# Sliding attention of block 2 with heads taken in pairs, skip factors loaded as rows, and other start addresses for block 2's tiles

## The chip, the core and the metric

One core of a Trainium2 chip runs the whole program. TensorE (PE; its weight loads are shown as PEld) multiplies, VectorE (DVE), ScalarE (ACT) and GpSimd (POOL) do the rest, and SyncE (SP) issues most of the weight transfers. SBUF is the on-chip memory of 128 partitions, PSUM the accumulators that TensorE writes. The metric is the device time of one launch in microseconds, the median of three runs.

## The reference

Block 1 is a mixer (mLSTM and differential attention) and a mixture of 32 experts; block 2 has two layers, each a gated feed-forward (ffn1), a mixer of three branches, and a second feed-forward (ffn2). Sequence 256, width 1024, fp32. The changed branch is the third one:

```python
def swa_sink_attention(q, k, v, sinks, band_bias, band_mask):   # 16 query heads, 2 key heads, width 64
    ...                                                          # blocks of 128 queries, window 128
    s = jnp.einsum('bnqkgd,bnskd->bnkgqs', q, kb) * (ATT_HEAD_DIM ** -0.5)
    s = jnp.where(band_mask[None, :, None, None], s + band_bias, NEG)
    m = jnp.maximum(jnp.max(s, axis=-1, keepdims=True), sink)
    e = jnp.exp(s - m)
    p = e / (jnp.sum(e, axis=-1, keepdims=True) + jnp.exp(sink - m))
    o = jnp.einsum('bnkgqs,bnskd->bnqkgd', p.astype(v.dtype), vb)
```

In the mixer, `ssd_mixer` adds `xs * d_skip` per head, and `x = x + rmsnorm(sum(sigmoid(gate) * (branch @ w_branch)) @ w_out)` closes it.

## The kernel before, in words

**Products.** Large products run in a single-pass format (fp32r): each operand is split into a high part (rounded by ACT) and a low part (the rest, by DVE), and three products are summed: high by high, high by low, low by high. Weights arrive in 1 MB pieces in the buffers `raw` or `fraw`; `split_to` makes `wh` and `wl` from them, four pairs of buffers deep. `wstat` holds a weight as the stationary operand and streams the 256 tokens (`xTH`, `xTL`, or a branch's output `yyH`, `yyL`, `yaq`, `yacsB`): a unit is 24 matmuls of 256 columns. `xstat` holds tokens and streams weights: matmuls of 512 columns, as in the second half of a feed-forward (`acc<-wh,fhH`) and in the heads of the stages (`mm<-own,xTH`). In a matmul's name `out<-a,b` a is streamed and b is stationary. Small products in full fp32 show as two records each.

**Order.** Every engine's order is the order in which the program is written. In the mixer a foreground loop of `wstat` units is interleaved with background generators (`ssd`, `swa`, `ret`, one after another). After each unit `bg` asks a running count of estimated TensorE, DVE and ACT work whether the first generator may go on by a step; `need` forces it on.

**`swa` before.** An item is (key head kv, query block b, half i): i picks partitions 0 to 63 or 64 to 127 of `aq` and `ak`, since two heads lie above each other. The eight items go through four stages, one step apart: `logits` (matmuls of one half, then DVE adds the band bias and takes the maximum), `exps` on ACT, `turn` (transposes on TensorE, ACT copies to `pT`, DVE the reciprocal of the sum), and `value` (the transposed weights stationary, 64 columns of `avr` streamed, DVE multiplies by the reciprocal into `ao`). At the end 16 transposes on TensorE turn `ao` over, and it is split into `yyH` and `yyL`. Stages take accumulators from `acc`, a ring of four PSUM banks.

**Addresses.** Each pool lays its tiles one behind another in SBUF, rounded up to 32 B. Small tiles (`dsk` 32 B, `hb` 192 B, `ssc` 16 B) thus set where the large ones behind them start. Start address modulo 128 B, in the program before: `wh`, `wl`, `raw` 64; `xTH`, `xTL` 0; `fhH`, `fhL`, `own`, `fhid` 32; `yyH` 64; `yyL`, `yaq`, `yacsB` 32.

Of the kernel before, what the change touches and what calls it, by code (L numbers as in the profile page):

```python
# [19 lines left out]
T = 256  # L20
NT = 2
D = 1024
# [117 lines left out]
class Kern:  # L140
# [477 lines left out]
    def block1(self):  # L618
        nc, tc, a = self.nc, self.tc, self.a
# [2 lines left out]
        xT = [self.mo.tile([128, KD, T], F32R, name="x" + t, tag=t, bufs=1) for t in ("XH", "XL")]  # L622
        self.boundary(self.w, None, None, self.g1, HL=xT)
        self.pump()
        vec1 = self.load_vecs(self.cp, [
            ("conv_w", a["conv_w"], 16), ("conv_b", a["conv_b"], 4), ("m_norm_g", a["m_norm_g"], 4),
            ("m_skip", a["m_skip"], 4), ("da_norm_g", a["da_norm_g"], 1)], "col1")
        scr = self.scr = self.w[:].rearrange("p t d -> p (t d)")
# [859 lines left out]
    def load_layer(self, l):  # L1488

        nc, a, p = self.nc, self.a, self.b2  # L1490
        v = self.load_vecs(p, [
            ("conv_w", a["conv_w_2"][l], 48), ("conv_b", a["conv_b_2"][l], 12), ("ssd_g", a["ssd_norm_g_2"][l], 8),
            ("gn_g", a["ret_gn_g_2"][l], 8), ("b_gate", a["b_gate_2"][l], 24)], f"col2_{l}")
        dsk = p.tile([128, 8], F32, name=f"dsk{l}")
        d = a["d_skip_2"]
        for i in range(2):
            nc.gpsimd.dma_start(dsk[i * 64:(i + 1) * 64],
                                bass.AP(tensor=d.tensor, offset=d.offset + l * 16 + i, ap=[[0, 64], [2, 8], [1, 1]]))
        hb = p.tile([128, 48], F32, name=f"hb{l}")
        for i, n in enumerate(("attn_sinks_2", "dt_bias_2", "a_log_2")):  # L1500
            nc.gpsimd.dma_start(hb[:, 16 * i:16 * i + 16], bcast(a[n][l], 16))
        yield
        c = self.vec_cols(v)
        for n in ("b_gate", "ssd_g", "gn_g"):
            nc.vector.tensor_scalar(c[n], c[n], 0.5, None, op0=OP.mult)
        sink = p.tile([128, 2, 2, 4], F32, name=f"sink{l}")
        for kv in range(2):
            nc.vector.tensor_copy(sink[:, kv], hb[:, 8 * kv:8 * kv + 8].rearrange("p (j i) -> p i j", i=2))
        nc.scalar.activation(hb[:, 32:48], hb[:, 32:48], AF.Exp)
        self.layer.append((c, dsk, sink, hb))  # L1510
        yield

    def setup2(self):
        nc, a, p = self.nc, self.a, self.b2
        self.rpow(self.q[:, 7], self.q[:, 4])
        for t in range(NT):
            nc.scalar.activation(self.x[:, t], self.x[:, t], AF.Copy, scale=self.q[:, 7, t:t + 1])
        cret = p.tile([128, 1544], F32, name="cret")
        nc.gpsimd.dma_start(cret[:], a["cret"])
        self.cosT, self.sinT = cret[:, 0:256], cret[:, 256:512]  # L1520
        self.dm = cret[:, 512:1024].rearrange("p (h i) -> p h i", h=4)
        self.xiB = cret[:, 1024:1536].rearrange("p (h i) -> p h i", h=4)
        self.zeta = cret[:, 1536:1540]
        yield
        for l in range(2):
            yield from self.load_layer(l)

    def mix(self, l):
# [7 lines left out]
        self.l = l  # L1536
# [97 lines left out]
        for m in (0, 2, 1):  # L1634
            if m == 0:
                self.need("ssd")
                mixed = p.tile([128, 8, T], F32, name="mixed", tag="xbc")
            if m == 2:
                self.need("kv1")
                self.rg = p.tile([128, 8, T], F32, name="rg", tag="rg")  # L1640
# [2 lines left out]
            for i in range(4):  # L1643
# [71 lines left out]
    def ssd(self):  # L1715
# [142 lines left out]
        self.rpow(vc[:, NT:], vc[:, 0:NT])  # L1858
        yield
        vb = p.tile([128, NT, 128], F32, name="ssv", tag="row2")  # L1860
        nc.vector.tensor_copy(vb[:], vc[:, NT:, None].to_broadcast([128, NT, 128]))
        yield
        pr = self.acc()
        for t in range(NT):
# [12 lines left out]
    def swa(self):  # L1877
# [14 lines left out]
        m = p.tile([128, 8, 6, 4], F32, name="am", tag="row1")  # L1892
        o = p.tile([128, 2, D], F32, name="ao", tag="xdt")
        ov = o[:].rearrange("p b (kv j i d) -> p b kv i j d", kv=2, j=4, i=2)

        def logits(n, kv, b, i):
            nk = 128 * (b + 1)
            lg, r = lgs[:, n % 2], slice(i * 64, (i + 1) * 64)
            for q in range(b + 1):
                ps = self.acc()  # L1900
                js = range(2 * q, 2 * q + 2) if b else range(4)
                for x, j in enumerate(js):
                    nc.tensor.matmul(ps[:, x * nk:(x + 1) * nk], self.aq[r, 4 * kv + j, b * 128:(b + 1) * 128],
                                     self.ak[r, kv, 0:nk], start=True, stop=True)
                for x, j in enumerate(js):
                    nc.vector.tensor_tensor_reduce(lg[:, j, :nk], ps[:, x * nk:(x + 1) * nk],
                                                   band[kv][:, i, j, T - nk:], 1.0, self.sink[:, kv, i, j:j + 1],
                                                   op0=OP.add, op1=OP.max, accum_out=m[:, n, 0, j:j + 1])
            nc.vector.tensor_scalar(m[:, n, 1], m[:, n, 0], -1.0, None, op0=OP.mult)
            nc.vector.tensor_sub(m[:, n, 2], self.sink[:, kv, i], m[:, n, 0])  # L1910

        def exps(n, kv, b, i):
            nk = 128 * (b + 1)
            lg = lgs[:, n % 2]
            nc.scalar.activation(m[:, n, 2], m[:, n, 2], AF.Exp)
            for j in range(4):
                nc.scalar.activation(lg[:, j, :nk], lg[:, j, :nk], AF.Exp, bias=m[:, n, 1, j:j + 1],
                                     accum_out=m[:, n, 3, j:j + 1])

        def turn(n, kv, b, i):  # L1920
            lg, pT = lgs[:, n % 2], pTs[:, n % 2]
            for kb in range(b + 1):
                ps = self.acc()
                for j in range(4):
                    nc.tensor.transpose(ps[:, j * 128:(j + 1) * 128], lg[:, j, kb * 128:(kb + 1) * 128], self.ident)
                nc.scalar.activation(pT[:, kb], ps[:], AF.Copy)
            nc.vector.tensor_add(m[:, n, 4], m[:, n, 3], m[:, n, 2])
            nc.vector.reciprocal(m[:, n, 5], m[:, n, 4])

        def value(n, kv, b, i):  # L1930
            pT = pTs[:, n % 2]
            ps = self.acc()
            for j in range(4):
# [7 lines left out]
        stages = (logits, exps, turn, value)  # L1941
        for n in range(len(items) + 3):
            for k in reversed(range(4)):
                if 0 <= n - k < len(items):
                    stages[k](n - k, *items[n - k])
                    if k:
                        yield 1
            yield
        self.flags.add("kv1")
        yield from self.wait(("br", 0))  # L1950
        H, L = self.yt("yH", "yL")
        for b in range(2):
            for g in range(2):
                ps = self.acc()
# [3 lines left out]
                s = slice(b * 128, (b + 1) * 128)  # L1958
                self.split_out(H[:, 4 * g:4 * g + 4, s], L[:, 4 * g:4 * g + 4, s],
                               ps[:].rearrange("p (k q) -> p k q", k=4))  # L1960
                yield 1
        self.yT[2] = (H, L)
        self.flags.add(("y", 2))

# [234 lines left out]
```

## Time and profile before

| | us |
|---|---|
| median of 3 runs (lowest, highest) | 2174.16 (2172.33, 2181.71) |
| the profiled execution, its own time | 2177.87 |
| its span, first to last instruction | 2176.1 |
| TensorE busy, DVE busy, ACT busy in it | 2089.0, 1109.1, 918.2 |

The mean granted clock of TensorE is 0.987 of full speed. Matmuls overlap in the records: each lasts about 280 ns for 256 columns while the next starts some 115 ns after it, so the pace is read from starts, or from how many fall into a stretch, and not from a record's length. The two mixers lie at about 903 to 1247 us and 1625 to 1996 us.

### The profile page before, as it was taken

How to read it: one execution, taken by the hardware profiler on the slowest of the kernel's cores; microseconds unless marked ns; L12 is line 12 of the kernel's file. 1: busy time of each engine (PE TensorE's matmuls, PEld its weight loads, DVE VectorE, ACT ScalarE, POOL GpSimd, SP SyncE). 2: the span in 40 equal slices, each digit the busy share in tenths (PEclk: the TensorE clock that was granted, in tenths of full speed). 3: DMA queues.
4: the chain of work that ended last, by engine and by line, in shares of the span. 5: the costliest groups of instructions: out<-in, count | busy, mean ns of one | idle time of the engine just before them, and what ended most of it. 6: DMA issues, size and time to landing. Idle time of an engine off the chain costs nothing. (4 is left out here: it accounts for less than half of the span.)

```text
span 2176.1 us, 33683 instructions
## 1 busy us (share of the span) xinstructions
PE 2089.0 (96%) x14031; PEld 1710.5 (79%) x14031; DVE 1109.1 (51%) x1778; ACT 918.2 (42%) x1420; POOL 95.1 (4%) x137
## 2 busy tenths in 40 slices
PE   8988999999887999999999999999999999999998
PEld 7864344433336997999999899899889999997996
DVE  5852111100115555777575665555558775756554
ACT  4441111111114544656544544444456555445442
POOL 3010000000002100000000100010000000001000
PEclk9988999999998999999999999999999999999999
DMA  8378999999996764656346475555546463455652
GB/s 252 117 281 322 384 414 416 415 416 417 420 384 186 183 221 158 197 159 213 98 144 225 136 252 194 194 193 178 191 143 208 146 212 108 156 194 183 214 195 76
DMA packets 265499, 500.05 MB, mean 230 GB/s; under 512 B 11868, under 2 KB 208940, under 8 KB 247040
## 3 DMA queue, kind: packets, MB, share of 16 engines
q1 hardware_dynamic: 258528, 474.88, 61.5%
q0 software_dynamic: 6816, 22.99, 3.6%
q8 instruction: 112, 1.84, 0.3%
q14 instruction: 43, 0.35, 0.1%
HBM read 494.62 MB, written 3.21 MB: 229 GB/s over the span
## 5 line engine op out<-in xcount | busy, mean ns | idle before, releaser
L125 PE MATMUL mm<-xTH,wh 128*128 128x256 f32 x2416 | 681.2, 282 | 4.7 <-ACT fhid L125 4.7
L125 PE MATMUL mm<-xTH,wl 128*128 128x256 f32 x2416 | 673.1, 279 | 3.6 <-DVE wl L125 3.6
L125 PE MATMUL mm<-xTL,wh 128*128 128x256 f32 x2416 | 672.5, 278 | 0.0
L125 DVE TENSOR_TENSOR wl<-raw,wh 128x1024 fp32r<-128x1024 f32 (+1 forms) x380 | 460.1, 1218 | 273.6 <-ACT wh L125 271.6
L125 ACT ACTIVATE wh<-raw 128x1024 fp32r<-128x1024 f32 (+1 forms) x380 | 396.4, 1051 | 221.1 <-PE mm L125 134.5
L125 PEld LDWEIGHTS mm<-xTH,wh 128*128 128x128 f32 x2416 | 455.5, 189 | 11.8 <-issue 5.0
L125 PEld LDWEIGHTS mm<-xTH,wl 128*128 128x128 f32 x2416 | 454.2, 188 | 5.3 <-DVE wl L125 4.7
L125 PEld LDWEIGHTS mm<-xTL,wh 128*128 128x128 f32 x2416 | 453.7, 188 | 2.0 <-issue 1.0
L125 DVE TENSOR_TENSOR wl<-fraw,wh 128x1024 fp32r<-128x1024 f32 x92 | 112.0, 1224 | 80.2 <-ACT wh L125 79.8
L125 DVE TENSOR_TENSOR hid<-mm,hid 128x512 f32<-128x512 f32 x16 | 11.1, 692 | 270.8 <-PE mm L125 270.8
L125 ACT ACTIVATE wh<-fraw 128x1024 fp32r<-128x1024 f32 x92 | 96.9, 1056 | 89.3 <-PE mm L125 47.7
L125 PE MATMUL acc<-wh,fhH 128*128 128x512 f32 x304 | 99.9, 397 | 0.0
L125 PE MATMUL acc<-wh,fhL 128*128 128x512 f32 x304 | 99.7, 396 | 0.0
L125 PE MATMUL acc<-wl,fhH 128*128 128x512 f32 x304 | 99.7, 396 | 0.0
L125 DVE SCALAR_TENSOR_TENSOR yhl<-mm,gs,yhl 128x512 fp32r<-128x512 f32 x32 | 24.0, 750 | 134.8 <-ACT yhl L125 133.6
L125 PE MATMUL mm<-raw,xg 128*64 128x512 f32 x264 | 77.7, 596 | 4.0 <-DMA raw<-in_w_eu_dram 4.0
L125 PE MATMUL mm<-rawB,xg 128*64 128x512 f32 x304 | 79.2, 596 | 1.0 <-DMA rawB<-in_w_eu_dram 1.0
L125 PE MATMUL mm<-yyH,wh 128*128 128x256 f32 x256 | 73.3, 286 | 0.0
L125 PE MATMUL mm<-yyL,wh 128*128 128x256 f32 x256 | 72.1, 282 | 0.0
L125 PE MATMUL mm<-yyH,wl 128*128 128x256 f32 x256 | 72.1, 282 | 0.0
L125 ACT ACTIVATE yhl<-mm,gs 128x512 fp32r<-128x512 f32 x32 | 22.0, 688 | 112.0 <-PE mm L125 110.0
L125 PEld LDWEIGHTS acc<-wh,fhL 128*128 128x128 f32 x304 | 57.3, 188 | 13.9
(532 smaller groups left out, 3284.1 us busy)
## 6 DMA issues: line engine op xcount, KB each, us to landing
raw<-in_w_in_dram SPq DMA_DIRECT2D x88, 1024.0 KB, 5.2
raw<-in_w_ffn_in_dram SPq DMA_DIRECT2D x52, 1024.0 KB, 5.6
fraw<-in_w_ffn_in_dram SPq DMA_DIRECT2D x28, 1024.0 KB, 6.8
raw<-in_w_ffn_out_dram SPq DMA_DIRECT2D x24, 1024.0 KB, 5.0
rawB<-in_w_eg_dram SPq DMA_DIRECT2D x23, 1024.0 KB, 13.8
rawB<-in_w_ed_dram SPq DMA_DIRECT2D x22, 1024.0 KB, 13.3
raw<-in_w_branch_dram SPq DMA_DIRECT2D x22, 1024.0 KB, 5.3
fraw<-in_w_ffn_out_dram SPq DMA_DIRECT2D x20, 1024.0 KB, 5.0
```

The lines of the kernel that those rows point to most:

```text
L125: return f(out, *args, **kw)
```

## The change

1. `swa`: an item is now (kv, b, q), with both halves i in it; for b = 0 all four j, for b = 1 two of them, so there are six items. `logits` issues the matmuls of the two halves alternately, into two accumulators. A new stage `norm` multiplies the exponentials by the reciprocal on DVE before the transposes. `value` now holds `avr` (64 columns wide) and streams `pT`, the two halves i going to output partitions 0 to 63 and 64 to 127. Its result stands already turned, DVE copies it, and the 16 transposes at the end are gone. A third buffer for the logits lies in the tile `mixed`, which `swa` now allocates; the mixer's loop forces `swa` on until it is there.
2. The skip factors come as a fourth row of `hb`, with one transfer of whole rows in place of two transfers of single values, and two DVE copies a layer.
3. Sizes are padded (`dsk`, `hb`, `cret`, `ssc`) and the vectors of block 1 move to another pool. Start addresses modulo 128 B after: `wh`, `wl`, `raw` 64 as before; `xTH`, `xTL` 0 as before; `fhH`, `fhL`, `own`, `fhid`, `yyH`, `yyL`, `yaq`, `yacsB` 0.

```diff
@@ block1
-        vec1 = self.load_vecs(self.cp, [
+        vec1 = self.load_vecs(p, [
@@ load_layer
-        dsk = p.tile([128, 8], F32, name=f"dsk{l}")
-        d = a["d_skip_2"]
-        for i in range(2):
-            nc.gpsimd.dma_start(dsk[i * 64:(i + 1) * 64],
-                                bass.AP(tensor=d.tensor, offset=d.offset + l * 16 + i, ap=[[0, 64], [2, 8], [1, 1]]))
-        hb = p.tile([128, 48], F32, name=f"hb{l}")
-        for i, n in enumerate(("attn_sinks_2", "dt_bias_2", "a_log_2")):
+        dsk = p.tile([128, 16], F32, name=f"dsk{l}")
+        hb = p.tile([128, 64], F32, name=f"hb{l}")
+        for i, n in enumerate(("attn_sinks_2", "dt_bias_2", "a_log_2", "d_skip_2")):
             nc.gpsimd.dma_start(hb[:, 16 * i:16 * i + 16], bcast(a[n][l], 16))
+        for i in range(2):
+            s = slice(i * 64, (i + 1) * 64)
+            nc.vector.tensor_copy(dsk[s, 0:8], hb[s, 48:64].rearrange("p (k i) -> p i k", i=2)[:, i])
@@ setup2, ssd
-        cret = p.tile([128, 1544], F32, name="cret")
+        cret = p.tile([128, 1552], F32, name="cret")
-        vc = p.tile([128, 2 * NT], F32, name="ssc")
+        vc = p.tile([128, 32], F32, name="ssc")
@@ mix
-                mixed = p.tile([128, 8, T], F32, name="mixed", tag="xbc")
+                    if m == 0:
+                        while self.mixed is None:
+                            self.bg(force=True)
+                        mixed = self.mixed
@@ swa
-        lgs = p.tile([128, 2, 4, T], F32, name="alg", tag="acsB", bufs=1)
+        self.mixed = p.tile([128, 12, T], F32, name="mixed", tag="xbc")
+        lgs = p.tile([128, 2, 1024], F32, name="alg", tag="acsB", bufs=1)
+        LG = [lgs[:, 0], lgs[:, 1], self.mixed[:, 8:12].rearrange("p a t -> p (a t)")]
...
-        def logits(n, kv, b, i):
-            for q in range(b + 1):
-                ps = self.acc()
-                js = range(2 * q, 2 * q + 2) if b else range(4)
-                for x, j in enumerate(js):
-                    nc.tensor.matmul(ps[:, x * nk:(x + 1) * nk], self.aq[r, 4 * kv + j, b * 128:(b + 1) * 128],
-                                     self.ak[r, kv, 0:nk], start=True, stop=True)
+        def logits(n, kv, b, q):
+            ps = [self.acc() for _ in range(2)]
+            for x, j in enumerate(js):
+                for i in range(2):
+                    r = slice(i * 64, (i + 1) * 64)
+                    nc.tensor.matmul(ps[i][:, x * nk:(x + 1) * nk], self.aq[r, 4 * kv + j, b * 128:(b + 1) * 128],
+                                     self.ak[r, kv, 0:nk], start=True, stop=True)
...
+        def norm(n, kv, b, q):
+            nc.vector.tensor_add(m[:, n, 2, s], m[:, n, 3, s], m[:, n, 2, s])
+            nc.vector.reciprocal(m[:, n, 3, s], m[:, n, 2, s])
+            nc.vector.tensor_mul(lg, lg, m[:, n, 3, s][:, :, None].to_broadcast([128, 2 * nj, nk]))
...
-        def value(n, kv, b, i):
-            for j in range(4):
-                for kb in range(b + 1):
-                    nc.tensor.matmul(ps[:, j * 64:(j + 1) * 64], pT[:, kb, j * 128:(j + 1) * 128],
-                                     vr[:, kb, kv * 64:(kv + 1) * 64], start=(kb == 0), stop=(kb == b))
-            nc.vector.tensor_mul(ov[:, b, kv, i], ps[:, 0:256].rearrange("p (j d) -> p j d", j=4),
-                                 m[:, n, 5][:, :, None].to_broadcast([128, 4, 64]))
+        def value(n, kv, b, q):
+            for kb in range(b + 1):
+                for i in range(2):
+                    nc.tensor.matmul(ps[i * 64:(i + 1) * 64, 0:w], vr[:, kb, kv * 64:(kv + 1) * 64],
+                                     pT[:, i, kb * w:(kb + 1) * w], start=(kb == 0), stop=(kb == b))
+            nc.vector.tensor_copy(o[:, j:j + nj, b * 128:(b + 1) * 128], ps[:, 0:w].rearrange("p (j q) -> p j q", j=nj))
-        items = [(kv, b, i) for kv in range(2) for b in range(2) for i in range(2)]
+        items = [(kv, *bq) for kv in range(2) for bq in ((0, 0), (1, 0), (1, 1))]
-        for b in range(2):
-            for g in range(2):
-                for k in range(4):
-                    nc.tensor.transpose(ps[:, k * 128:(k + 1) * 128], o[:, b, (4 * g + k) * 128:(4 * g + k + 1) * 128],
-                                        self.ident)
...
+        for q in range(4):
+            s = slice(2 * q, 2 * q + 2)
+            self.split_out(H[:, s], L[:, s], o[:, s])
```

TensorE in the first layer's mixer, before, between two units of the foreground: one step of `value`, `turn` and `logits` (here `c_82` is the identity of a transpose, and `mm` rows are foreground).

```order
L125 MATMUL mm<-xTH,wl 128x256
L125 MATMUL acc<-avr,pT 128x64 x8
L125 MATMUL acc<-c_82,alg 128x128 x8
L125 MATMUL acc<-ak,aq 128x128 x4
L125 MATMUL mm<-yyH,wh 128x256
```

The same step after the change:

```order
L125 MATMUL mm<-xTH,wl 128x256
L125 MATMUL acc<-pT,avr 64x512 x2
L125 MATMUL acc<-c_82,alg 128x128 x8
L125 MATMUL acc<-ak,aq 128x256 x4
L125 MATMUL mm<-xTH,wh 128x256
```

Two wide matmuls stand where eight narrow ones did. In a layer there are 32 `ak,aq` matmuls before and after (16 of each width), 48 `avr,pT` before and 20 `pT,avr` after, 48 transposes of `alg` or `mixed` both times, and 16 transposes of `ao` before and none after. One item's `logits` now also come before the first `yyH` unit.

DVE around one `value`, before:

```order
L125 TENSOR_TENSOR wl<-raw,wh 128x1024
L125 TENSOR_TENSOR ao<-acc,am 128x4x64
L125 TENSOR_TENSOR am<-am 128x4
L125 RECIPROCAL am<-am 128x4
L125 ISA alg,am<-acc,band,sink_4902 128x256
```

And after, at the first `value` of the layer:

```order
L125 TENSOR_TENSOR wl<-raw,wh 128x1024
L125 COPY ao<-acc 128x4x128
L125 TENSOR_TENSOR am<-am 128x4
L125 RECIPROCAL am<-am 128x4
L125 TENSOR_TENSOR mixed<-mixed,am 128x1024
L125 ISA alg,am<-acc,band,sink_4901 128x256
```

The multiplication of 1024 columns is new on DVE, and the copy that follows `value` is twice as wide as the multiplication before.

## Rows read from the trace of the kernel before

**Rows 1.** The page: TensorE's busy time, and what its largest group waited for.

```profile
PE 2089.0 (96%) x14031; PEld 1710.5 (79%) x14031; DVE 1109.1 (51%) x1778; ACT 918.2 (42%) x1420; POOL 95.1 (4%) x137
L125 PE MATMUL mm<-xTH,wl 128*128 128x256 f32 x2416 | 673.1, 279 | 3.6 <-DVE wl L125 3.6
```

**Rows 2.** Busy times by stretch: first mixer; then its attention, 1025 to 1085.

```profile
core 0: us, PE busy (x) PEld busy (x) DVE busy (x) ACT busy (x) POOL busy (x), PEclk, DMA share, GB/s
900.00:1250.00 350.00, 347.01 (x2745) 328.75 (x2744) 239.25 (x432) 187.28 (x317) 15.44 (x17) 1.00 0.52 169
1025.00:1085.00 60.00, 60.00 (x474) 56.38 (x474) 33.20 (x117) 34.38 (x101) 0.00 (x0) 1.00 0.32 101
```

**Rows 3.** TensorE's instructions in order of time, in the first layer's attention.

```profile
start us, us, engine line op out<-in xcount [idle before <-releaser]
1029.00 1.16 PE L125 MATMUL acc<-ak,aq 64*128 64x128 f32 x8
...
1033.56 1.99 PE L125 MATMUL acc<-ak,aq 64*128 64x256 f32 x8
1035.48 0.39 PE L125 MATMUL mm<-yyH,wh 128*128 128x256 f32 x1
...
1050.40 1.89 PE L125 MATMUL acc<-avr,pT 128*128 128x64 f32 x16
1052.13 0.72 PE L125 MATMUL acc<-c,alg 128*128 128x128 f32 x5
...
1087.72 1.91 PE L125 MATMUL acc<-c,ao 128*128 128x128 f32 x16
1089.39 0.36 PE L125 MATMUL mm<-xTH,wh 128*128 128x256 f32 x1
```

**Rows 4.** The same view where halves of the array alternate: block 1, then `ssd`.

```profile
86.64 2.09 PE L125 MATMUL acc<-hT 64*128 64x256 f32 x16
...
121.91 1.16 PE L125 MATMUL mm<-hT 64*128 64x128 f32 x16
...
947.73 0.66 PE L125 MATMUL acc<-acsB,xdt 128*64 128x128 f32 x8
```

**Rows 5.** DVE's groups from 1025 to 1085.

```profile
L125 DVE TENSOR_TENSOR wl<-raw,wh 128x1024 fp32r<-128x1024 f32 x11 | 13.5, 1224 | 8.9 <-ACT wh L125 8.6
L125 DVE CUSTOM_DVE_ANT_0 alg<-acc,band,sink 128x128 f32<-128x128 f32 x16 | 4.7, 347 | 5.6 <-PE acc L125 5.6
L125 DVE TENSOR_TENSOR ao<-acc,am 128x256 f32<-128x256 f32 x8 | 3.4, 424 | 7.0 <-PE acc L125 7.0
```

**Rows 6.** TensorE where units on `yyH`, `yyL` alternate with units on `xTH`, `xTL`.

```profile
1147.53 0.28 PE L125 MATMUL mm<-yyH,wh 128*128 128x256 f32 x1
...
1153.22 0.28 PE L125 MATMUL mm<-xTH,wh 128*128 128x256 f32 x1
...
1158.68 0.28 PE L125 MATMUL mm<-yyH,wh 128*128 128x256 f32 x1
```

**Rows 7.** Stretches of one kind of matmul: ffn1 and ffn2 of layer 2, ffn2's second half.

```profile
1446.00:1546.00 100.00, 100.00 (x852) 100.00 (x851) 56.45 (x55) 47.67 (x56) 0.00 (x0) 1.00 0.63 206
2010.00:2100.00 90.00, 90.00 (x797) 90.00 (x796) 53.22 (x52) 44.59 (x51) 0.00 (x0) 1.00 0.65 211
2108.00:2148.00 40.00, 40.00 (x172) 32.17 (x171) 22.04 (x19) 18.26 (x18) 0.00 (x0) 1.00 0.37 131
```

**Rows 8.** TensorE's matmuls of 512 columns: twelve up to `ssv`, and heads.

```profile
999.23 0.39 PE L125 MATMUL mm<-wh,xTH 128*128 128x512 f32 x1
...
1001.97 0.49 PE L125 MATMUL acc<-c,ssv 128*128 128x128 f32 x3
...
1234.28 2.03 PE L125 MATMUL mm<-own,xTH 128*128 128x512 f32 x8
...
1237.08 2.03 PE L125 MATMUL mm<-own,xTH 128*128 128x512 f32 x8
```

**Rows 9.** The tile `band`: its issue on POOL's timeline; its view's time to landing.

```profile
1000.94 1.46 POOL L1882 DMA_DIRECT2D band<-bandD  x2
...
DMA to landing us min/median/max: 6.0/8.4/9.5
```

More of the change, by code (lines that the diff above doesn't have):

```diff
@@ L1517, in setup2 @@
             nc.scalar.activation(self.x[:, t], self.x[:, t], AF.Copy, scale=self.q[:, 7, t:t + 1])
-        cret = p.tile([128, 1544], F32, name="cret")
-        nc.gpsimd.dma_start(cret[:], a["cret"])
+        cret = p.tile([128, 1552], F32, name="cret")
+        nc.gpsimd.dma_start(cret[:, :1544], a["cret"])
         self.cosT, self.sinT = cret[:, 0:256], cret[:, 256:512]
@@ L1535, in mix @@
         self.bgs, self.yT, self.flags, self.later = [], {}, set(), []
-        self.l = l
+        self.l, self.mixed = l, None
         self.bgall, self.bgps = False, self.acc
@@ L1855, in ssd @@
                                  start=(k == 0), stop=(k == 1))
-        vc = p.tile([128, 2 * NT], F32, name="ssc")
+        vc = p.tile([128, 32], F32, name="ssc")
         nc.vector.tensor_scalar(vc[:, 0:NT], ps[:, 0:NT], 1.0 / D, 1e-6, op0=OP.mult, op1=OP.add)
-        self.rpow(vc[:, NT:], vc[:, 0:NT])
+        self.rpow(vc[:, NT:2 * NT], vc[:, 0:NT])
         yield
         vb = p.tile([128, NT, 128], F32, name="ssv", tag="row2")
-        nc.vector.tensor_copy(vb[:], vc[:, NT:, None].to_broadcast([128, NT, 128]))
+        nc.vector.tensor_copy(vb[:], vc[:, NT:2 * NT, None].to_broadcast([128, NT, 128]))
         yield
@@ L1889, in swa @@
             yield
-        lgs = p.tile([128, 2, 4, T], F32, name="alg", tag="acsB", bufs=1)
+        self.mixed = p.tile([128, 12, T], F32, name="mixed", tag="xbc")
+        lgs = p.tile([128, 2, 1024], F32, name="alg", tag="acsB", bufs=1)
+        LG = [lgs[:, 0], lgs[:, 1], self.mixed[:, 8:12].rearrange("p a t -> p (a t)")]
         pTs = p.tile([128, 2, 2, 512], F32, name="pT", tag="cmd", bufs=1)
-        m = p.tile([128, 8, 6, 4], F32, name="am", tag="row1")
-        o = p.tile([128, 2, D], F32, name="ao", tag="xdt")
@@ L1894, in swa @@
-        ov = o[:].rearrange("p b (kv j i d) -> p b kv i j d", kv=2, j=4, i=2)
-        def logits(n, kv, b, i):
-            nk = 128 * (b + 1)
-            lg, r = lgs[:, n % 2], slice(i * 64, (i + 1) * 64)
-            for q in range(b + 1):
-                ps = self.acc()
-                js = range(2 * q, 2 * q + 2) if b else range(4)
-                for x, j in enumerate(js):
-                    nc.tensor.matmul(ps[:, x * nk:(x + 1) * nk], self.aq[r, 4 * kv + j, b * 128:(b + 1) * 128],
-                                     self.ak[r, kv, 0:nk], start=True, stop=True)
[L1905 to L1915, printed above, removed]
-            for j in range(4):
[L1917 to L1921, printed above, removed]
-            for kb in range(b + 1):
-                ps = self.acc()
[L1924 to L1928, printed above, removed]
@@ L1930, in value @@
-        def value(n, kv, b, i):
-            pT = pTs[:, n % 2]
-            ps = self.acc()
-            for j in range(4):
-                for kb in range(b + 1):
-                    nc.tensor.matmul(ps[:, j * 64:(j + 1) * 64], pT[:, kb, j * 128:(j + 1) * 128],
-                                     vr[:, kb, kv * 64:(kv + 1) * 64], start=(kb == 0), stop=(kb == b))
-            nc.vector.tensor_mul(ov[:, b, kv, i], ps[:, 0:256].rearrange("p (j d) -> p j d", j=4),
-                                 m[:, n, 5][:, :, None].to_broadcast([128, 4, 64]))
@@ L1940, in swa, with dims @@
-        items = [(kv, b, i) for kv in range(2) for b in range(2) for i in range(2)]
-        stages = (logits, exps, turn, value)
-        for n in range(len(items) + 3):
-            for k in reversed(range(4)):
+        m = p.tile([128, 6, 4, 8], F32, name="am", tag="row1")
+        o = p.tile([128, 8, T], F32, name="ao", tag="xdt")
+        def dims(b, q):
+            nk, js = 128 * (b + 1), range(2 * q, 2 * q + 2) if b else range(4)
+            return nk, js, len(js)
+        def logits(n, kv, b, q):
+            nk, js, nj = dims(b, q)
+            lg = LG[n % 3].rearrange("p (h k) -> p h k", k=nk)
+            ps = [self.acc() for _ in range(2)]
[5 more added lines that the diff above has]
+            for i in range(2):
+                for x, j in enumerate(js):
+                    h = i * nj + x
+                    nc.vector.tensor_tensor_reduce(lg[:, h], ps[i][:, x * nk:(x + 1) * nk],
+                                                   band[kv][:, i, j, T - nk:], 1.0, self.sink[:, kv, i, j:j + 1],
+                                                   op0=OP.add, op1=OP.max, accum_out=m[:, n, 0, h:h + 1])
+            nc.vector.tensor_scalar(m[:, n, 1, :2 * nj], m[:, n, 0, :2 * nj], -1.0, None, op0=OP.mult)
+            nc.vector.tensor_sub(m[:, n, 2, :2 * nj].rearrange("p (i j) -> p i j", i=2),
+                                 self.sink[:, kv, :, js[0]:js[0] + nj],
+                                 m[:, n, 0, :2 * nj].rearrange("p (i j) -> p i j", i=2))
@@ new lines, in exps @@
+        def exps(n, kv, b, q):
+            nk, js, nj = dims(b, q)
+            lg = LG[n % 3].rearrange("p (h k) -> p h k", k=nk)
+            nc.scalar.activation(m[:, n, 2, :2 * nj], m[:, n, 2, :2 * nj], AF.Exp)
+            for h in range(2 * nj):
+                nc.scalar.activation(lg[:, h], lg[:, h], AF.Exp, bias=m[:, n, 1, h:h + 1],
+                                     accum_out=m[:, n, 3, h:h + 1])
+        def norm(n, kv, b, q):
+            nk, js, nj = dims(b, q)
+            lg, s = LG[n % 3].rearrange("p (h k) -> p h k", k=nk), slice(0, 2 * nj)
+            nc.vector.tensor_add(m[:, n, 2, s], m[:, n, 3, s], m[:, n, 2, s])
+            nc.vector.reciprocal(m[:, n, 3, s], m[:, n, 2, s])
+            nc.vector.tensor_mul(lg, lg, m[:, n, 3, s][:, :, None].to_broadcast([128, 2 * nj, nk]))
@@ new lines, in turn @@
+        def turn(n, kv, b, q):
+            nk, js, nj = dims(b, q)
+            lg, pT = LG[n % 3].rearrange("p (h k) -> p h k", k=nk), pTs[:, n % 2]
+            for i in range(2):
+                ps = self.acc()
+                for kb in range(b + 1):
+                    for x in range(nj):
+                        c = kb * nj + x
+                        nc.tensor.transpose(ps[:, c * 128:(c + 1) * 128], lg[:, i * nj + x, kb * 128:(kb + 1) * 128],
+                                            self.ident)
+                nc.scalar.activation(pT[:, i], ps[:], AF.Copy)
@@ new lines, in value @@
+        def value(n, kv, b, q):
+            nk, js, nj = dims(b, q)
+            pT, w = pTs[:, n % 2], nj * 128
+            ps = self.acc()
+            for kb in range(b + 1):
+                for i in range(2):
+                    nc.tensor.matmul(ps[i * 64:(i + 1) * 64, 0:w], vr[:, kb, kv * 64:(kv + 1) * 64],
+                                     pT[:, i, kb * w:(kb + 1) * w], start=(kb == 0), stop=(kb == b))
+            j = 4 * kv + js[0]
+            nc.vector.tensor_copy(o[:, j:j + nj, b * 128:(b + 1) * 128], ps[:, 0:w].rearrange("p (j q) -> p j q", j=nj))
@@ L1944, in swa @@
+        items = [(kv, *bq) for kv in range(2) for bq in ((0, 0), (1, 0), (1, 1))]
+        stages = (logits, exps, norm, turn, value)
+        for n in range(len(items) + 4):
+            for k in reversed(range(5)):
                 if 0 <= n - k < len(items):
@@ L1951, in swa @@
         H, L = self.yt("yH", "yL")
-        for b in range(2):
-            for g in range(2):
-                ps = self.acc()
-                for k in range(4):
-                    nc.tensor.transpose(ps[:, k * 128:(k + 1) * 128], o[:, b, (4 * g + k) * 128:(4 * g + k + 1) * 128],
-                                        self.ident)
[L1958 to L1961, printed above, removed]
+        for q in range(4):
+            s = slice(2 * q, 2 * q + 2)
+            self.split_out(H[:, s], L[:, s], o[:, s])
+            yield 1
         self.yT[2] = (H, L)
```

## Prediction

> **What bounds the kernel now.** I read the page first. TensorE is busy for 2089 of 2176 us, and its largest group waited 3.6 us in all for the DVE that makes its weights [rows 1]. [...] So in block 2 the time is the length of TensorE's own stream: an instruction taken out of it, or a faster pace of it, shortens the run one for one, until DVE or a buffer falls behind. The rest is read from starts in the order of time, since records overlap.
>
> **Attention, per layer.** *Logits.* Before, a step with eight records of 128 columns takes 1.16 us, of which 0.07 lies under the next instruction, as at the 256-column step (1.99 long, the next start 1.92 later) [rows 3]. There are four of each: 4 x 1.09 + 4 x 1.92 = 12.0 us. These use one half of the array's rows at a time. Block 1 alternates the halves in the way that the new code does: sixteen records of 128 columns take the same 1.16 us, and sixteen of 256 take 2.09 where eight take 1.99 [rows 3, 4]. So the new steps cost 1.09 (twice) and, as half of 2.09 with a little that does not halve, 1.1 (four times): 6.6 us, a gain of 5.4.
>
> *Value.* Before, sixteen records of 64 columns take 1.73 us from start to start (1050.40 to 1052.13) [rows 3]; four steps of that and four of half, 10.4 us. After there are six steps, each with 1024 streamed columns (two matmuls of 512, or four of 256), in pairs on two halves of the output columns. The nearest row has four matmuls of 128 columns in such pairs, 512 columns in 0.66 us [rows 4]. Twice the columns cost between 0.66 (if it were all drain) and 1.32 (if none were); I take 1.0, since part of it is drain. Six steps: 6.0, a gain of 4.4 (bounds 2.5 and 6.4).
>
> *Turning over.* The 16 transposes of `ao` go: 1087.72 to 1089.39, 1.7 us [rows 3]. The 48 others stay. Sum 5.4 + 4.4 + 1.7 = 11.5 us a layer, 23.0 in two.
>
> *What it adds.* On DVE, six multiplications of 1024 columns (the split of the same size takes 1.22 us) and six copies of 512 columns (0.42 at 256, so about 0.7) in place of eight multiplications at 0.42 [rows 5]: 7.3 + 4.2 - 3.4, less some 1.3 for two items' small operations, +6.8 us a layer. DVE goes from 33 of 60 to about 40 of 49 us, 82% [rows 2]. That is hidden under TensorE as long as the splits keep their lead of three units, over 8 us; the longest new burst, eight maxima at 0.35 and one multiplication, is 4 us, so I take nothing. Without that cover the last rival applies. A wait is added: `value` takes one accumulator, `turn` two, `logits` two, five from a ring of four. Where all three stand in one step (twice a layer, see the order), the second half of `logits` waits until DVE has copied `value` out. Behind it on TensorE stands the foreground. DVE may have a split in front, so the copy comes up to 1.2 + 0.7 us after `value`; the 8 transposes in between cover 0.8 [rows 3, 5]. Four such places at 0 to 1.1 us, I take 0.5 each: +2. The first maxima now come before the first `yyH` unit, roughly 9 us earlier than before. They read `band`, issued at 1000.94 with at most 9.5 us to landing, so it lies there by 1012 [rows 9]: nothing. Attention in all: -21 us (bounds -27 and -9, the latter if the halves did not overlap).
>
> **Start addresses.** Where branch units alternate with gate units, 48 matmuls streaming `yyH` and `yyL` (64 and 32 B past a multiple of 128) take 5.69 us, and 48 streaming `xTH` and `xTL` (at 0) take 5.46, with the same weight buffers at 64 [rows 6]. All 1152 such matmuls would gain 24 x 0.23 = 5.5; about two thirds stand in this regular alternation, the others between attention steps, so I take 3.7. In a feed-forward's second half, weights at 64 stream against `fhH`, `fhL` at 32: 172 in 40 us, two of which only reach into the stretch, so 235 ns each. With the stationary operand at 0 the twelve matmuls up to `ssv` take 2.74 us, 228 ns [rows 7, 8]. I take 5 ns for 912 of them: 4.6. The 240 matmuls of `own` (at 32) against `xTH`, `xTL` take 2.80 us a dozen, 233 ns [rows 8]; both at 0 afterwards, and a combination that these rows do not show. I take the same 5 ns: 1.2. Together -9.5 (bounds below).
>
> What speaks against it is a stretch of equal addresses at two paces: 100 us of ffn1 hold 852 `xT` matmuls, 90 us of ffn2 hold 797, 117 against 113 ns, at the same clock [rows 7]. The pace thus has a cause beside the addresses. If both ffn2 stages took the slow one, 2 x 864 x 4.4 ns = +7.6 us; if both ffn1 stages took the fast one, -7.6. With that the addresses' part lies between -17 and +8.
>
> [...]
>
> **Skip factors, padding.** POOL issues two transfers fewer, DVE gets four copies of 8 columns, each below the 0.35 us of a 128-column operation [rows 5], in ffn1 of layer 1, a stage like the one where DVE is busy for 56 of 100 us [rows 7]. Nothing. If that cover were gone, 1.4 us.
>
> **The sum.** -21 - 9.5 = -30.5 us. The profiled execution took 2177.87 us (1.8 around its span), which gives 2147.4. It lies 3.7 above the median of the runs, 2174.16; on the median the forecast is 2143.7, say 2144.
>
> **Rivals.** All times stand on the median. *The addresses do nothing*, and attention alone counts: 2174 - 21 = 2153. For it speaks the unexplained second pace, against it rows 6. *The pace of the long `xT` stretches changes* with the new addresses of their neighbours: fast in all of them, 2144 - 7.6 = 2136; slow in all, 2151. For it: the two paces [rows 7]; against it: neither `xT` nor `wh` moves against the 128 B. *The halves do not overlap*, so that the pairs do not do what they are written for: logits stay at 12.0, +10.9 in both layers, 2155; rows 4 speak against it twice. *Slower than before:* the transposes of an item now stand behind DVE's `norm`. If, at each of the 12 items, TensorE arrives with a split, eight maxima and the multiplication still to do (1.2 + 2.8 + 1.2 = 5.2 us), it waits. It decides from 30.5 / 12 = 2.5 us an item; at 4 us an item it gives 2144 + 48 = 2192. For it speaks DVE at 82%, against it that between `norm` and `turn` of an item there is always at least one foreground unit of 24 matmuls, some 2.8 us, and that DVE has caught up with TensorE at each maximum (it waited 5.6 us for the accumulators of the narrow ones [rows 5]).
>
> **How the numbers follow.** Forecast 0.45; addresses nothing 0.27; fast pace 0.13, slow pace 0.07; halves 0.04; slower 0.04. The range leaves out the last and the outer ends of the others: down to 2128 (fast pace, no waits at the ring, value steps near 0.66), up to 2160 (no help from addresses, with waits at their upper bound). A change of this kernel can be told from none from about 0.5%, 11 us, on. Faster by more holds in all cases but the last and a part of the halves' case: 0.94; within 0.03; slower 0.03.
>
> **What would show it.** Right: `ak,aq` steps with sixteen records of 128 columns in about 1.16 us and eight of 256 in about 1.1; `pT,avr` steps near 1.0; no `c,ao`; branch units at 5.46 us for 48; some 175 matmuls `acc<-wh,fhH` and its kin in 40 us; the attention stretch shorter by 11 us a layer and TensorE still busy throughout. Wrong: gaps on TensorE in front of `alg` transposes or of `ak,aq` that are ended by DVE; steps of 1.9 us for eight records of 256; the long `xT` stretches at another pace; starts at 0 that still show 235 ns. The forecast fails if the total moves by less than 11 us, or if the attention stretch gives less than half of its 21.

## The result, and the profile after

The changed kernel took 2140.24 us (median of 4 runs, 2139.20 to 2143.21) beside 2173.24 us before (2170.09 to 2181.71): ratio 0.9837, 95% interval [0.9815, 0.9859]. The profiled spans are 2176.1 and 2138.4 us. The forecast was 2144, from 2128 to 2160. The size came out; its make-up only in part.

The page after, answering [rows 1]: 144 matmuls fewer, TensorE still busy for 96%.

```profile
PE 2055.6 (96%) x13887; PEld 1672.6 (78%) x13887; DVE 1120.0 (52%) x1774; ACT 917.2 (43%) x1416; POOL 93.2 (4%) x135
L125 PE MATMUL mm<-xTH,wl 128*128 128x256 f32 x2416 | 671.0, 278 | 3.2 <-DVE wl L125 3.2
```

Busy times of the first mixer and of its attention, answering [rows 2]:

```profile
core 0: us, PE busy (x) PEld busy (x) DVE busy (x) ACT busy (x) POOL busy (x), PEclk, DMA share, GB/s
887.00:1237.00 350.00, 345.81 (x2762) 324.05 (x2762) 252.31 (x437) 193.27 (x323) 15.43 (x17) 1.00 0.55 178
1013.00:1060.00 47.00, 47.00 (x383) 40.68 (x382) 36.28 (x97) 29.75 (x81) 0.00 (x0) 1.00 0.36 114
```

TensorE in order of time in the changed attention, answering [rows 3]. DVE's copy and multiplication there, answering [rows 5], stand under it.

```profile
start us, us, engine line op out<-in xcount [idle before <-releaser]
1003.84 1.16 PE L125 MATMUL acc<-ak,aq 64*128 64x128 f32 x16
1004.93 0.39 PE L125 MATMUL mm<-yyH,wh 128*128 128x256 f32 x1
...
1010.78 1.13 PE L125 MATMUL acc<-ak,aq 64*128 64x256 f32 x8
1011.85 0.39 PE L125 MATMUL mm<-xTH,wh 128*128 128x256 f32 x1
...
1029.33 1.08 PE L125 MATMUL acc<-pT,avr 128*64 128x512 f32 x4
1030.34 1.09 PE L125 MATMUL acc<-c,alg 128*128 128x128 f32 x8
...
1031.36 1.45 PE L125 MATMUL acc<-ak,aq 64*128 64x256 f32 x8
1032.74 0.38 PE L125 MATMUL mm<-xTH,wh 128*128 128x256 f32 x1
```

```profile
L125 DVE TENSOR_TENSOR alg<-alg,am 128x1024 f32<-128x1024 f32 x4 | 4.9, 1225 | 0.1
L125 DVE COPY ao<-acc 128x512 f32<-128x512 f32 x2 | 1.4, 684 | 0.0
```

From start to start the logits take 1.09 and 1.07 us, a value step 1.01. Where `value`, `turn` and `logits` share a step, the logits take 1.38 (the row at 1031.36), 0.31 more: the wait for an accumulator. DVE is busy for 36.3 of 47 us (77%), and TensorE never stops.

Where branch units alternate with gate units, answering [rows 6], the pairs `yyH`, `yyL` take 5.62 us for 48 matmuls, the pairs `yaq`, `yacsB` 5.44, as `xTH`, `xTL` do:

```profile
1113.12 0.28 PE L125 MATMUL mm<-yyH,wh 128*128 128x256 f32 x1
...
1118.74 0.28 PE L125 MATMUL mm<-xTH,wh 128*128 128x256 f32 x1
...
1146.30 0.28 PE L125 MATMUL mm<-yaq,wh 128*128 128x256 f32 x1
...
1151.74 0.28 PE L125 MATMUL mm<-xTH,wh 128*128 128x256 f32 x1
```

The stretches of one kind, answering [rows 7] (ffn1 and ffn2 of layer 2, ffn2's second half): ffn1 has gone over to the quick pace, the second half holds one matmul more.

```profile
1423.00:1513.00 90.00, 90.00 (x797) 90.00 (x796) 53.25 (x52) 44.55 (x51) 0.00 (x0) 1.00 0.63 207
...
1970.00:2060.00 90.00, 90.00 (x796) 90.00 (x796) 52.49 (x52) 44.65 (x53) 0.00 (x0) 1.00 0.66 217
2070.00:2110.00 40.00, 40.00 (x173) 32.31 (x172) 21.85 (x19) 18.05 (x18) 0.00 (x0) 1.00 0.38 131
```

Stage by stage, from the start of one kind of matmul to that of the next (first `c,fhid` to first `wh,fhH`; `c,avT` to `rqk`; `rqk` to `wh,yyH`), us, in the profiled executions; e1 to e4 are the first four experiments:

| stage | before | after | e1 | e2 | e3 | e4 |
|---|---|---|---|---|---|---|
| ffn1, layer 1, first half | 110.3 | 99.1 | 107.1 | 100.9 | 102.0 | 107.1 |
| attention, layer 1 | 78.9 | 70.6 | 71.0 | 78.5 | 78.9 | 70.7 |
| rest of mixer, layer 1 | 116.6 | 113.1 | 113.8 | 115.8 | 116.6 | 113.1 |
| ffn2, layer 1, first half | 98.4 | 98.4 | 98.4 | 98.4 | 102.2 | 98.4 |
| ffn1, layer 2, first half | 102.2 | 98.4 | 98.4 | 98.4 | 98.4 | 98.4 |

Layer 2's mixer repeats layer 1's within 0.1. From before to after one foreground unit of 24 `xT` matmuls, some 2.8 us, has moved from the rest of the mixer into the attention stretch (240 `xT` matmuls there in place of 216), so the two rows are best read as a sum. Of the 37.7 us between the profiled spans, 23.8 stand in the two mixers, and 15.1 in two feed-forward halves in which the change edits no matmul.

The larger of these, 11.3 us in ffn1 of layer 1, is for the most part a hole in the kernel before, in which TensorE waits and then runs at a lower clock (some 8 us; the other 3 are the slow pace, as e3 and e4 show below). Its waits from 680 to 715 (engine, line, releaser: us in total, times, longest), then TensorE's rows around the hole:

```profile
PE mm L125 <- ACT fhid L125: 4.7, 1, 4.7
```

```profile
694.77 0.28 PE L125 MATMUL mm<-xTH,wl 128*128 128x256 f32 x1
699.72 0.58 PE L125 MATMUL mm<-xTH,wh 128*128 128x256 f32 x1 [4.67 <-ACT fhid L125]
700.09 0.42 PE L125 MATMUL mm<-xTL,wh 128*128 128x256 f32 x1
```

After 4.7 us of idling the matmuls run at about half the pace for a while, 0.21 us from start to start in place of 0.12 ahead of the hole: the granted clock is 1.00 up to 698, 0.94 from there to 699, 0.50 from 699 to 705, 0.64 to 706, and 1.00 again from there on. ACT, named as the releaser, stood itself behind the split of a weight that landed late. The rows are that split, then the weight's transfer (issued at 678.36) and the two `dsk` transfers of 4-byte elements (issued at 682.04 and 682.77), with KB each and median us from issue to landing; the last row is the same weight in the changed kernel:

```profile
697.63 1.06 ACT L125 ACTIVATE wh<-raw 128x1024 fp32r<-128x1024 f32 x1 [13.13 <-DMA raw<-in_w_ffn_in_dram]
...
raw<-in_w_ffn_in_dram SPq DMA_DIRECT2D x1, 1024.0 KB, 19.2
...
dsk<-in_d_skip_dram POOLq DMA_DIRECT2D x2, 2.0 KB, 11.8
...
raw<-in_w_ffn_in_dram SPq DMA_DIRECT2D x1, 1024.0 KB, 6.5
```

The weight was issued 3.7 us ahead of the `dsk` transfers and landed at 697.53, 0.3 us behind the second of them. All transfers from 684 to 698 (busy tenths and GB/s in forty slices of 0.35 us):

```profile
DMA  9989989999000007799799970001233467999999
GB/s 453 409 344 432 415 303 345 244 98 13 0 0 32 29 26 24 33 85 39 9 1 1 1 0 0 0 6 35 76 114 120 140 243 274 388 326 353 347 361 345
```

From 687 to 694 no more than 85 GB/s pass. The tenths put the whole time of a packet into the slice in which it starts, and stop at 9, so a 0 behind a 9 need not be an idle engine. From 691.1 to 692.1 POOL's queue starts these packets (number, MB, share of the 16 engines' time in that 1 us):

```profile
q0 software_dynamic: 10, 0.00, 258.5%
```

Each of the ten thus took 4.1 us. The trace has 32 packets of this kind, of 128 B and so 4 KB in all, as much as the two `dsk` transfers: sixteen start from 686.4 to 687.3 and sixteen from 689.5 to 692.1, and they take 1.7 to 4.7 us each, where a 1 KB packet of a weight takes 0.05. All five traces with the old transfers have them, in both layers; none of the nine traces without does. The second layer's pair (issued at 745.86) leaves 112 and 68 GB/s over 740 to 750 and 750 to 760, but TensorE is busy throughout. The changed kernel, 683 to 697:

```profile
DMA  9999998656898999999999999999999999999999
GB/s 391 441 379 348 333 220 116 81 76 173 258 288 293 332 389 380 383 383 398 380 382 383 372 385 392 386 410 357 363 366 357 377 336 363 345 348 339 328 322 322
```

Here 258 to 410 GB/s pass from 686.5 on, beside 0 to 85 from 687 to 694 in the kernel before.

### The profile page after: what moved, and what is told of

It reads as the page before. It is cut to its first block, busy times and chain, and to the rows that moved or that the text cites. A ratio compares the mean times of both kernels' runs of the same rounds, so it can differ in the third digit from the quotient of the medians.

```text
span 2138.4 us, 33376 instructions
## 1 busy us (share of the span) xinstructions
PE 2055.6 (96%) x13887; PEld 1672.6 (78%) x13887; DVE 1120.0 (52%) x1774; ACT 917.2 (43%) x1416; POOL 93.2 (4%) x135
```

## The experiments

Theory after the result: attention gives what was forecast, the starts less, the skip factors the hole, and the pace of the long `xT` stretches has a cause of its own. Rivals: the starts set that pace; the hole was an accident.

**e1, attention alone.** The changed kernel less all else:

```diff
-        cret = p.tile([128, 1552], F32, name="cret")
+        cret = p.tile([128, 1544], F32, name="cret")
...
+            nc.gpsimd.dma_start(dsk[i * 64:(i + 1) * 64],
+                                bass.AP(tensor=d.tensor, offset=d.offset + l * 16 + i, ap=[[0, 64], [2, 8], [1, 1]]))
```

> The kernel before with the paired attention alone; skip factors and every start address as before. Theory: attention gives 8.3 us a layer, 17 us in all, ratio 0.992; the other 16 us of the measured gain stay away. In its trace ak,aq steps near 1.1 us and pT,avr steps near 1.0 us, yyH units still at 5.69 us for 48 matmuls, and in ffn1 of layer 1 a gap of TensorE of 4 to 5 us near 700 us, ended by a late weight transfer. Rival A (the rest of the mixer is shorter because of the new order of attention, not because of the starts): ratio 0.988, yyH units below 5.6 us. Rival B (the gap in ffn1 was an accident of one execution): no gap.

2149.91 us (2145.27 to 2161.14), ratio 0.9901 [0.9873, 0.9928]. By stages attention gives 7.9 and the rest of the mixer 2.9 a layer: 21.6 us in two. The second part is the foreground unit that has moved into the attention stretch, so attention itself gives 10.8 a layer; the 17 of the expectation left that out. Of Rival A the order of attention is right and the sign is not: the `yyH` units still take 5.69 us. The hole is there (4.1 us).

**e2, starts alone.** The kernel before with the paddings and the moved vectors.

```diff
-        vc = p.tile([128, 2 * NT], F32, name="ssc")
+        vc = p.tile([128, 32], F32, name="ssc")
```

> The kernel before with the new start addresses alone (paddings, and the first block's vectors in another pool); attention and the two skip-factor transfers of 4-byte elements per layer as before. Theory: 3.9 us a layer in the mixers, 8 us in all, ratio 0.996, yyH units at 5.45 to 5.62 us for 48; the gap in ffn1 stays. The pace of the long xT stretches (113 or 118 ns) is not set by these starts, so either may show. Rival (the starts also set the pace of ffn1): 113 ns in both ffn1 stages, ratio 0.993. Rival (the addresses do nothing): ratio 1.000, yyH units at 5.69 us.

2162.18 us, ratio 0.9943 [0.9925, 0.9961]; more than expected, and within 2.9 us over six runs. The mixers give only 2.4 us. The rest stands in ffn1: no slow pace in layer 2, and no hole, though the transfers of 4-byte elements are there. Here the weight that the hole waited for had landed before their packets started (686.14 and later):

```profile
raw<-in_w_ffn_in_dram SPq DMA_DIRECT2D x1, 1024.0 KB, 6.0
```

It was issued at 678.34 and landed at 684.30; in the kernel before, issued at 678.36, at 697.53. In the four traces with the hole (before, e1, e4, e11) it lands 0.2 to 0.6 us behind the second `dsk` transfer. So the transfers alone don't make the hole: in these five traces it came where the weight that TensorE needed next was still under way when their packets started, and stayed away where it had landed 1.8 us earlier. Why it was quicker in e2 was not found.

**e3, skip factors alone,** and **e4, the changed kernel with the old transfers.** e3 fetches them as a row:

```diff
-                                bass.AP(tensor=d.tensor, offset=d.offset + l * 16 + i, ap=[[0, 64], [2, 8], [1, 1]]))
+        nc.gpsimd.dma_start(raw, bcast(a["d_skip_2"][l], 16))
```

> The kernel before with the skip factors fetched as one row of 16 for all partitions, landed in the tile of the sinks and copied from there; no tile's size or address changes. Theory: the two transfers of 4-byte elements hold up the weights in ffn1 of layer 1, TensorE waits 4.7 us there and runs at half the clock for 3 us behind it; without them both go, 7.8 us, ratio 0.9965, and the gap is missing in the trace. Rival (the gap was an accident of one execution and the edit is hidden, as the prediction had it): ratio 1.000.

> The changed kernel with the old transfers of skip factors (two per layer, of 4-byte elements), addresses as in the changed kernel. Theory: the gap comes back in ffn1 of layer 1, some 5 us of wait and 3 us at half the clock, so 2148 us, ratio to the kernel before 0.988. Rival (the edit is hidden): 2140 us, ratio 0.985, no gap of TensorE above 1 us between 680 and 720 us.

e3: 2171.45 us, ratio 0.9978 [0.9961, 0.9996]; e4: 2149.04, ratio 0.9874 [0.9851, 0.9896]. Busy times of TensorE from 690 to 710, e3 first, then e4:

```profile
690.00:710.00 20.00, 20.00 (x172) 1.00 0.98 310
```

```profile
690.00:710.00 20.00, 14.36 (x107) 0.91 0.92 276
```

The hole goes with the row fetch and comes back with the old one (4.3 us of wait); the rival falls. e3's profiled span is 7.3 us shorter than before, with 3.8 lost again to the slow pace in ffn2 of layer 1 (table); by the medians it gains 3, the old transfers cost the changed kernel 9. One run of e4 took 2139.35, as quick as the changed kernel, so the hole is probably not in every execution; that run has no trace. Over all fourteen traces, four of the five with the old transfers have a wait of 2.9 to 4.7 us there, and none of the nine without has one above 0.8.

**e5, logits one half after the other.**

```diff
-            for x, j in enumerate(js):
-                for i in range(2):
+            for i in range(2):
+                for x, j in enumerate(js):
```

> The changed kernel with the logits of an item issued one row half after the other, in place of in turn. Theory (the gain of the logits is the overlap of two row halves): ak,aq steps of eight records of 256 columns go from 1.06 us back to near 2.0, and those of sixteen of 128 columns from 1.09 to near 2.0, less the one place in a step where the halves still meet; 3.5 to 5 us a layer, 2148 to 2150 us, ratio 0.988. Rival (it came from fewer instructions and less drain): unchanged, 2140 us, ratio 0.985.

2142.62 us, ratio 0.9856 [0.9829, 0.9883]. Between the two: the narrow step is dearer by half, the wide one not.

```profile
1003.00 1.71 PE L125 MATMUL acc<-ak,aq 64*128 64x128 f32 x16
1004.64 0.39 PE L125 MATMUL mm<-yyH,wh 128*128 128x256 f32 x1
...
1010.50 1.14 PE L125 MATMUL acc<-ak,aq 64*128 64x256 f32 x8
1011.57 0.39 PE L125 MATMUL mm<-xTH,wh 128*128 128x256 f32 x1
```

1.64 us in place of 1.09, and 1.07 as before; 1.2 us a layer. The narrow step shows that taking turns matters where a half has four matmuls (eight records); with two a half the order costs nothing, and why was not settled.

**e6, all of block 2 at 32 again; e7, `yyH` 128 B later; e8, all of it 128 B later.** One number each:

```diff
-        cret = p.tile([128, 1552], F32, name="cret")
+        cret = p.tile([128, 1560], F32, name="cret")   # e6; e8: 1584
...
-        vc = p.tile([128, 32], F32, name="ssc")
+        vc = p.tile([128, 64], F32, name="ssc")        # e7
```

> The changed kernel with 32 B of padding behind the constants, so that every tile of block 2 behind them starts 32 B past a multiple of 128 again. Theory (the starts set the pace of Y units, and make the slow pace of the long xT stretches more likely): yaq units from 5.44 back to 5.67 us, 2.4 us in both mixers, and single stretches of ffn at 118 in place of 113 ns, 3.8 us each, in some executions: 2142.5 to 2148 us, with over 6 us between the lowest and the highest. Rival (the pace of the long stretches has nothing to do with the starts): 2142.5 us within 4 us, all long stretches at 113 ns.

> The changed kernel with 128 B of padding ahead of yyH alone, which then starts 128 B past a multiple of 256 as xTH, xTL, yyL and yaq do. Theory (of two multiples of 128 B only the odd ones give the pace of 113 ns beside the weights as they lie): the yyH units go from 5.62 us for 48 matmuls to 5.44, 768 such matmuls, 3 us, 2137 us, ratio 0.982. Rival (a multiple of 128 is all that counts, and yyH is slow for another reason): 2140 us, yyH units at 5.62 us.

> The changed kernel with 128 B of padding behind the constants: every tile of block 2 behind them moves by 128 B, so yaq and its partner from odd to even multiples of 128, yyH from even to odd and yyL from odd to even; xTH and xTL stay. Theory (odd multiples are fast): yaq units go from 5.44 to about 5.62 us for 48, the mixed pair yyH, yyL stays near 5.62; 1.5 us more, 2141.5 us, ratio 0.985. Rival (what counts is that the two tiles of a pair lie equally against 256 B): yaq stays at 5.44 us. Rival (any multiple of 128 does): all units as in the changed kernel.

e6: 2151.55 us, ratio 0.9890 [0.9862, 0.9917], 12.6 us between lowest and highest, three of four long stretches slow and the `yaq` units back at 5.67 us, all as the theory has it but for a median above its range. e7: 2141.24, 0.9846 [0.9820, 0.9873]; e8: 2144.31, 0.9863 [0.9836, 0.9889]; in time neither stands apart from the changed kernel, in the trace both do. In e7 all units take 5.44 us:

```profile
1114.78 0.28 PE L125 MATMUL mm<-yyH,wh 128*128 128x256 f32 x1
...
1120.22 0.28 PE L125 MATMUL mm<-xTH,wh 128*128 128x256 f32 x1
```

In e8, with `yaq` at an even multiple of 128, it takes 5.65, and the `xT` units between, on tiles that have not moved, take 5.65 too, which the theory did not foresee:

```profile
1159.02 0.28 PE L125 MATMUL mm<-yaq,wh 128*128 128x256 f32 x1
...
1164.67 0.28 PE L125 MATMUL mm<-xTH,wh 128*128 128x256 f32 x1
...
1170.32 0.28 PE L125 MATMUL mm<-yaq,wh 128*128 128x256 f32 x1
```

For the branch outputs the odd multiples of 128 are the quick ones; both rivals of e8 fall. These are the two paces of the long stretches again: 48 times 113.3 ns is 5.44 us, 48 times 117.8 is 5.65. The stationary `fhH`, `fhL`, now odd, also speed up: 176 matmuls in 40 us (2073 to 2113), 228.9 ns from start to start in place of 233.3, in three of the four second halves; in that of ffn1 in layer 1 they stay at 233.3, and why is open.

**e9, everything odd; e10, `fhid` alone at 32; e11, the kernel before with `fhid` alone at a multiple of 128; e12, the changed kernel again.**

```diff
+        p.tile([128, 8], F32, name="padA")    # e10; e11: 24
         hid0 = p.tile([128, NT, 256], F32, name="fhid0", tag="fhid", bufs=3)
+        p.tile([128, 56], F32, name="padB")   # e10; e11: 8
```

(e9 has the paddings of e7 and e8 and one of 128 B behind the tile `dts`.)

> The changed kernel with three paddings that put every operand of block 2's fast-format matmuls at an odd multiple of 128 B: fhH, fhL (from even to odd), yyH (from even to odd), while yaq, yacsB, yyL stay odd. Theory (odd multiples are fast, sizes from the two runs with shifts): fhH matmuls of 512 columns from 233.2 to 229.5 ns, 912 of them, 3.4 us; yyH units from 5.62 to 5.44 us, 2.5 us as measured: 6 us less than the changed kernel, some 2134 to 2135 us. Rival (the two do not add up, or the long stretches take the slow pace): no better than the changed kernel.

> The changed kernel with fhid alone 32 B past a multiple of 128, as it was before; all other operands as in the changed kernel. fhid is read by eight transposes per feed-forward stage, at its beginning. Theory (these transposes set the pace of the xT stretch behind them, and from a start of 32 they can leave it slow): in at least one of the four stages the pace goes from 113 to 118 ns right behind the transposes, 3.8 us each; 2141 to 2150 us with over 5 us between the lowest and the highest. Rival (another tile of the block, or chance, does it): all four at 113 ns behind the transposes, 2140 us within 4 us.

> The kernel before with fhid alone at a multiple of 128 B; its other operands stay at 32. Theory (the transposes set the pace): all four long xT stretches at 113 ns behind the transposes, 2 x 3.8 us less than the profiled execution of the kernel before: 2166 us, ratio 0.9965, and the runs closer together but for the gap in ffn1. Rival: single stretches at 118 ns behind the transposes as before, ratio 1.000.

> The changed kernel itself once more, as the measure of the other three on the same chip: 2140 us, ratio 0.985, and behind the transposes of fhid all four long xT stretches at 113 ns.

(The trace shows four such transposes per stage, not eight.) e9: 2138.55 us, 0.9830 [0.9814, 0.9846]; e10: 2147.32, 0.9869 [0.9852, 0.9886]; e11: 2170.69, 0.9980 [0.9964, 0.9995]; e12: 2138.04, 0.9836 [0.9819, 0.9852]. Long `xT` stretches, 90 us each, of ffn2 in layer 1, ffn1 and ffn2 in layer 2; e10, then e11:

```profile
1245.00:1335.00 90.00, 90.00 (x797) 1.00 0.62 208
1430.00:1520.00 90.00, 90.00 (x796) 1.00 0.63 208
1977.00:2067.00 90.00, 90.00 (x767) 1.00 0.62 209
```

```profile
1260.00:1350.00 90.00, 90.00 (x796) 1.00 0.66 217
1446.00:1536.00 90.00, 90.00 (x797) 1.00 0.64 214
2006.00:2096.00 90.00, 90.00 (x797) 1.00 0.64 212
```

In e10 the pace changes at the `fhid` transposes in all four stages (quick to slow, slow to quick, slow to quick, quick to slow). Over all traces: with `fhid` at 32 it changed at 16 of 20 such places, ten of them to the slow side; with `fhid` at a multiple of 128, in nine traces of eight kernels, it was quick behind all 36. So this one tile's start decides whether the stretch behind it can turn slow, and the rival falls. Not all of e10's 9 us is that: beside e12 its profiled execution is 3.8 us longer in ffn2 of layer 2 and 1.3 in ffn1 of layer 1, and 7.2 ahead of block 2's first `xT` matmul, in code that the edit doesn't touch (the changed kernel's own two traces differ by 3.3 there). e11 gains 3 of the 7.6 us expected. In ffn1 of layer 1 the pace also changes further on, in every trace, and mostly where another transpose stands: at 14 of 28 places with the single transposes `mm<-c,col_0r` and `mm<-c,col_1r`, and at four other places. In the changed kernel it goes from 113.3 to 117.8 ns at 775.2, though the tile read there starts at a multiple of 128. So that start does not keep the pace quick for every tile; what does is open.

e9 is no better than the changed kernel. Its units and `fh` matmuls are as quick as expected (176 in 40 us, 5.44 us; 0.9 us less in each mixer and in three of the four second halves), 4.5 us in all, but beside e12 the heads between second mixer and ffn2, ffn1 of layer 1 and the attention stretches took back 3.4; by what is open. One tile goes the other way: in e11 the streamed `own` of a second half moves from 32 to 160 past a multiple of 256, `fhH` stays, and `acc<-own,fhH` goes from 227.1 to 232.5 ns.

## Why the prediction was right, and where it was not

- *Attention, -21.* Right: 21.6 by e1. Logits 6.6 forecast, 2 x 1.09 + 4 x 1.07 and 0.5 of waits measured; value steps 1.0, measured 1.01 (the records last 1.08, beside 0.66 for half the columns [rows 4], so they did not double with them; that the rest is drain, as the forecast took it, no run shows). The wait for an accumulator, 2 us at four places, came to 1.0 (0.31 and 0.17 a layer). DVE's addition, +6.8 us a layer in the forecast, came to 5.4 (1109.1 to 1120.0 in both) and stayed hidden; the forecast took all six copies as 512 wide, and four are 256.
- *Halves.* That they overlap holds; e5 puts 1.2 us a layer on the order in which they are issued.
- *Starts, -9.5.* The step that failed: "I take 5 ns for 912 of them: 4.6", and the same 5 ns for `own`. A multiple of 128 B is not what divides quick from slow; for most of these tiles odd or even against 256 B does (e7 to e9: a branch output's 48 matmuls 5.44 us at an odd multiple of 128, 5.62 to 5.65 at an even one; `fh` matmuls 228.9 and 233.3 ns). `fhH`, `fhL` went to an even multiple: 0.9 ns each in place of 5, some 0.1 us a second half. `own` in the heads gained 1.6 ns (234.0 to 232.4). `yyH` went to an even one too: 5.62, so that only the `yaq` pairs reached 5.44. In the mixers 2.4 us (e2) in place of 3.7. The row that gave the 5 ns was unfit: those twelve matmuls took 2.80 us in the changed kernel (2.74 in [rows 8]), with their operands placed against 256 B as before.
- *The rival of the quick pace,* held at 0.13, came in beside the forecast: 3.8 us in ffn1 of layer 2, some 3 in ffn1 of layer 1. In ffn1 of layer 2 its cause is a start after all, that of `fhid`, which the prediction had not looked at, since it asked what the slow matmuls read and not what ran just before them.
- *Skip factors, 0.* Failed, by about 8 us where the hole occurs. I priced the instructions on POOL and DVE and named DVE as the cover; the cost sat in the DMA engines, which the weights share: 32 packets of 128 B, up to 4.7 us each.
- *The others.* No wait behind `norm`, no slower case; the first maxima, at 1005.03, waited for TensorE alone, not for `band`.

So -30.5 against -37.7 between the profiled executions (-33.0 between the medians) hides three misses: 7 too much for the starts, and nothing for a hole of 8 and a pace of 7 (attention gave 0.6 more, and in all the rest 1.7 us net went the other way, most of it in the heads ahead of the last ffn2). The forecast was right on its largest term, and lucky in the sum of the others.

## What to carry to other kernels

Price a small transfer by what its packets do to the DMA engines when a weight is under way beside it, not by its bytes or its instruction: here 4 KB in 4-byte elements cost some 8 us where the hole occurred, and the row fetch left no hole (e3). Where like matmuls run at two paces, look at what runs just before the change of pace (here the `fhid` transposes), and try starts against 256 B, one tile at a time (`yyH` alone: 5.62 to 5.44 us for 48 matmuls, e7). Trust such a rule for the tile on which it was measured: `own` went against it (227.1 to 232.5 ns, e11). A unit of work on half of the array was worth pairing with one on the other half here: eight records of 256 columns took 1.92 us on one half [rows 3] and 1.07 on two.

## What the runs showed of the hardware that was not expected

- Matmuls of 256 columns with fast-format operands run at 113.3 or 117.8 ns at the same starts and the same granted clock (1.00), and keep a pace for up to 100 us. Four transposes of a tile at 32 B past a multiple of 128 changed it 16 times in 20; from a multiple of 128 it was always quick behind them (36 places).
- A streamed branch output at an even multiple of 128 B slows its own units: 5.62 to 5.65 us beside 5.44. In e8 (`yaq`) it slows the `xT` units between them too, to 5.65; in the changed kernel (`yyH`) these stay at 5.44.
- Two transfers of 4-byte elements, 4 KB in all, ran as 32 packets of 1.7 to 4.7 us each and kept everything on the 16 DMA engines at or under 85 GB/s for 7 us. A weight issued 3.7 us ahead of them landed 0.3 us behind them.
- Two half-array matmuls on one half, then two on the other, took 1.07 us, as in turn; four and four took 1.64 in place of 1.09.
